# One decoder layer on one core: in the first segment, keys and values transposed by TensorE, and 1/rms applied as results leave PSUM

## The chip, the cores and the metric

The kernel runs on one core of one Trainium2 chip. Five engines of the core have a queue each and work it off in order: TensorE (PE in the profile, with its weight loads as PEld), VectorE (DVE), ScalarE (ACT), GpSimd (POOL) and SyncE (SP), which here only issues DMAs. Matmul results land in PSUM, everything else lives in SBUF. The metric is the device time of one launch in microseconds.

## The reference

One layer, 2048 tokens, width 1024. The input is normalised, projected once, split into two groups of heads that each run a chunked recurrence, gated, and projected back:

```python
h = rms_norm(x, attn_norm)                      # x * rsqrt(mean(x*x) + EPS) * gain
proj = h @ w_in                                 # 1024 -> 8216 columns
(mq, mk, mv, mo, mz, mi, mf, gqkv, gz, gb, ga) = split(proj)
h_m = mlstm_chunkwise(q_m, k_m, v_m, i_pre, f_pre)          # 4 heads, q/k 128, v 256
y_m = rms(h_m) * sigmoid(mo) * silu(mz)
qkv = silu(causal_depthwise_conv(gqkv, g_conv))             # 8 heads of 128, conv of 4 taps
q_g, k_g, v_g = l2_norm(gq), l2_norm(gk), gv
o_g = gated_delta_chunkwise(q_g, k_g, v_g, log_alpha, beta) # triangular solve per chunk, state 128x128
y_g = rms(o_g) * silu(gz)
x = x + concat(y_m, y_g) @ w_out
out = rms_norm(x, final_norm)
```

What matters here: every projection of the normalised input is the projection of (x times gain) multiplied by one number per token, 1/rms. It can be multiplied into the input before, or into the result after. And the gated-delta heads need keys and values both with the channel on the partitions (as the projection and the convolution give them) and with the token on the partitions (for the state update), so they are transposed.

## The kernel before

The tokens go in four **segments** of 512, each of four chunks of 128. A segment is eight **windows**, written out in `ORDER`: P0, M0, P1, M1, P2, M2, P3, M3. A P window projects queries, keys, values and gate of a pair of gated-delta heads (`g_proj`), an M window those of one mLSTM head (`m_proj`). The generator `window` takes the steps of these projections as a filler and puts between them, at given fractions of the window, the steps of other streams: `prep` of pair n (the chunk matrices and a 32-step forward substitution) in window M n; `level` (building the 128x128 inverse), the first part of `chain` (the recurrence over the chunks) of pair n and `m_chunks` of head n in window P n+1; the rest of `chain` in window M n+1. PE runs in exactly the order in which the program is written. On DVE, ACT, POOL and SP a scheduler sets the order, from priorities and a simulated timeline of its own.

Every product of a projection is three passes (`hi*hi + hi*lo + lo*hi` of fp32 split in two). `proj_fm` (L337) makes 128 columns of a weight with the channel on the partitions, one PSUM tile of 128x512 from three buffers of `psj`; `proj_tm` (L365) makes 256 columns with the token on the partitions, four tiles of 128x256. In the first segment the weights come raw from HBM and are split on the way: a cast on ACT (L175) and a subtraction on POOL (L177), and both halves are written back to HBM, from where the other segments load them.

Also in the first segment alone, `raw[0]` is true: `hh` and `hl` hold x times gain without 1/rms. The result is therefore multiplied while it stands in PSUM, and read out after that: in `proj_fm` by DVE with `rbc0` (L348, 1/rms broadcast along the partitions), in `tm_done` by ACT with the column `rs0` (L361). Then the consumer reads PSUM: `keep_v` copies the mLSTM values to `mv` on ACT (L508) and DVE makes the low half `vlo` (L511); `conv_silu` copies to `xin` on ACT (L662), makes the first tap on ACT from PSUM (L664) and the other three on DVE (L666); `mq` and `mk` are copied on ACT (L498, L499); `mo` goes through tanh on ACT (L515).

The tables `VT` and `KTR` say for each segment (first, middle ones, last) and pair who transposes: 1 means DVE, in 16 blocks of four 32x32 transposes each for a head (`to_tokens`, L484), directly behind `conv_silu`, for the values (`gv`) and the keys (`ktok`); 0 means PE, four or two 128x128 transposes at a time into PSUM tiles of the pool `psc` (5 buffers), for the keys in `g_prep` (`ktp`, L736, read by ACT for the squares and a copy, L739 and L741) and for the values in `g_chain` (`vp`, L919, read by ACT, L921). Both go through `by_dve`. In the first segment pair 0 has 0 in both tables, pairs 1 to 3 have 1.

Names that come later: `dmz`, `zp`, `fp`, `zq`, `E` belong to `level`; `SS` is the state of the recurrence, `sp`, `vq`, `su`, `op` are its matmuls; `pts` and `kws` are split operands of `m_chunks`, `CN` and `nd` its state and output; `kl` are low halves for `prep`.

Of the kernel before, what the change touches and what calls it, by code (L numbers as in the profile page):

```python
# [10 lines left out]
F32 = mybir.dt.float32  # L11
# [40 lines left out]
VT = ((0, 1, 1, 1), (1, 1, 1, 1), (1, 0, 0, 0))  # L52
KTR = ((0, 1, 1, 1), (1, 1, 1, 1), (0, 1, 0, 0))
# [12 lines left out]
def hybrid_layer(  # L66
# [160 lines left out]
    rs0 = cst.tile([P, NCH], F32, name="rs0")  # L227
    rbc0 = cst.tile([P, T], F32, name="rbc0")
# [109 lines left out]
    def proj_fm(w, c0, nm, done):  # L338
# [3 lines left out]
        for k in range(KT):  # L342
# [3 lines left out]
            if k == KT - 1:  # L346
                if raw[0]:
                    nc.vector.tensor_tensor(ps, ps, rbc0, op=ALU.mult)  # L348
                done(ps)
# [9 lines left out]
    def tm_done(ps, t, done):  # L359
        if raw[0]:  # L360
            nc.scalar.activation(ps, ps, AF.Copy, scale=rs0[:, t:t + 1])  # L361
        done(ps, t)

    def proj_tm(w, nm, done):

        n = w[0][0].shape[-1]
        for t in range(NCH):
            ps = psj.tile([P, T], F32, tag="pj", name=f"pt_{nm}_{t}")[:, 0:n]
            for k in range(KT):
                tm_step(ps, w, t, k)  # L370
# [117 lines left out]
    def m_proj(seg, n, r):  # L488
# [9 lines left out]
                           lambda ps: nc.scalar.activation(qT, ps, AF.Copy, scale=DK ** -0.5))  # L498
        yield from proj_fm(w, P, f"mk{s_}", lambda ps: nc.scalar.copy(kT, ps))  # L499
# [6 lines left out]

        def keep_v(ps, t):
            nc.scalar.copy(vt[:, t, 0:256], ps)  # L508
            if fast:
                with tc.high_priority(VPR):  # L510
                    nc.vector.tensor_tensor(vlo[:, t, :], ps, vt[:, t, 0:256].bitcast(F32),  # L511
                                            op=ALU.subtract)
        yield from proj_tm(w, f"mv{s_}", keep_v)
        w = next_w()
        yield from proj_tm(w, f"mo{s_}", lambda ps, t: nc.scalar.activation(  # L515
            G[:, t, :], ps, AF.Tanh, scale=0.5))
# [133 lines left out]
    def g_proj_qkv(seg, pr, r):  # L650
        s_ = f"{seg}_{pr}"
        for part, tag in ((1, "gk"), (0, "gq"), (2, "gv")):
            w = next_w()
            for j in range(2):
# [715 lines left out]
```

## Time and profile before

| what | value |
|---|---|
| time, median of 3 runs | 2358.06 us (2354.9 to 2360.65) |
| profiled execution, its own time | 2354.22 us |
| span of its trace | 2352.2 us |
| PE busy | 2225.8 us (95%), 14750 matmuls |
| DVE busy | 1925.3 us (82%) |
| ACT busy | 876.1 us (37%) |
| POOL busy | 714.5 us (30%) |

The page's slices of the span read: PE 8 and 9 tenths from the start on and 9 everywhere behind the first quarter; DVE between 7 and 9; the granted clock 9 tenths in the first slices. The first segment ends at 534.5 us, where the projection `pt_gz` of the second one starts. Its windows begin at 7.5 (P0), 67.2 (M0), 134.4 (P1), 206.3 (M1), 265.9 (P2), 335.7 (M2), 395.6 (P3) and 465.5 us (M3); those of the second segment at 534.5, 603.0, 662.2, 724.1, 779.3, 836.5, 891.2 and 948.3 us. A view by stretches over these bounds gives one line for a window, with the busy time of each engine and the granted clock as a share of full speed.

### The profile page before, as it was taken

The numbers are of one execution on the slowest core, as the hardware profiler recorded it, in microseconds if no ns is written. First come the engines' busy times: TensorE is split into PE (matmuls) and PEld (weight loads), VectorE is DVE, ScalarE is ACT, GpSimd is POOL, SyncE is SP. The second block draws the span as 40 slices with busy tenths as digits, with TensorE's granted clock in tenths as the row PEclk, the third lists the DMA queues.
The fourth block names the chain that finished last, engine by engine and source line by source line (L and its number), as shares of the span: only waits on it lengthen the run. The fifth ranks groups of instructions, "written<-read, shape, count | busy, mean of one in ns | idle before, by whom it ended". The sixth has DMA issues, their size and how long they took to land.

```text
span 2352.2 us, 41574 instructions
## 1 busy us (share of the span) xinstructions
PE 2225.8 (95%) x14750; PEld 1970.7 (84%) x14750; DVE 1925.3 (82%) x5359; ACT 876.1 (37%) x2351; POOL 714.5 (30%) x820
## 2 busy tenths in 40 slices
PE   8889899889899999998999999999999999999998
PEld 7778788788789898887898989888988997777777
DVE  7989898996988888879888888788766837988784
ACT  5535454544333434343333343443334234111111
POOL 4435353451302121413020214130212114444433
PEclk9889999999999999999999999999999999999999
DMA  7766657574445554645454556454546455222221
GB/s 254 249 204 233 233 188 245 184 267 156 163 155 182 171 194 168 223 155 174 155 182 158 191 176 232 146 182 157 183 169 205 166 194 159 73 99 90 99 81 63
DMA packets 183320, 409.18 MB, mean 174 GB/s; under 512 B 51736, under 2 KB 84632, under 8 KB 183112
## 3 DMA queue, kind: packets, MB, share of 16 engines
q1 hardware_dynamic: 182392, 405.74, 50.9%
q8 instruction: 116, 1.90, 0.3%
q14 instruction: 92, 0.75, 0.1%
q10 hardware_dynamic: 720, 0.79, 0.1%
HBM read 309.68 MB, written 96.90 MB: 173 GB/s over the span
## 4 chain that ended last, share of the span: by engine, by line
PE 45%; DVE 37%; DMA 6%; issue 5%; ACT 3%; POOL 3%; SPq 0%; POOLq 0%; ACTq 0%; DVEq 0%
DVE ytt L1185 6%; DVE ktok L484 3%; DVE tb L816 3%; DVE xb L820 3%; DVE gv L484 2%; DVE kw L484 2%; PE pt_mz L355 2%; PE pt_mz L356 2%; PE pt_mz L357 2%; PE pt_mo L355 2%; PE pt_mo L356 2%; PE pt_mo L357 2%; PE pt_gz L356 2%; PE pt_gz L355 2%; PE pt_gz L357 2%
## 5 line engine op out<-in xcount | busy, mean ns | idle before, releaser
L1185 DVE STREAM_TRANSPOSE ytt<-yl 32x256 f32<-32x256 f32 x448 | 195.1, 436 | 42.0 <-POOL ylo L1153 35.9
L816 DVE TENSOR_TENSOR tb<-xb,lbt 128x248 f32<-128x248 f32 (+30 forms) x496 | 181.2, 365 | 20.5 <-DMA lbt<-l_d 7.7
L820 DVE TENSOR_TENSOR xb<-xb,tb 128x248 f32<-128x248 f32 (+30 forms) x496 | 172.0, 347 | 12.7
L983 POOL TENSOR_TENSOR gms<-gms,nhalf 128x2 f32<-128x2 f32 x64 | 46.8, 730 | 421.9 <-DVE gms L981 421.5
L355 PE MATMUL pt_mv<-whi_M,hh 128*128 128x256 f32 x512 | 149.3, 292 | 12.4 <-DVE vlo L511 8.3
L355 PE MATMUL pt_gz<-whi_P,hh 128*128 128x256 f32 (+1 forms) x512 | 153.8, 300 | 2.8 <-ACT whi_P L175 1.7
L355 PE MATMUL pt_mz<-whi_M,hh 128*128 128x256 f32 x512 | 150.1, 293 | 5.6 <-DVE tz L522 4.8
L355 PE MATMUL pt_mo<-whi_M,hh 128*128 128x256 f32 x512 | 149.4, 292 | 4.3 <-DVE vlo L511 4.3
L357 PE MATMUL pt_gz<-whi_P,hl 128*128 128x256 f32 (+1 forms) x512 | 148.3, 290 | 1.5 <-DVE mr L630 1.5
L356 PE MATMUL pt_gz<-wlo_P,hh 128*128 128x256 f32 (+1 forms) x512 | 148.4, 290 | 1.4 <-DVE wlo_P L177 1.4
L356 PE MATMUL pt_mv<-wlo_M,hh 128*128 128x256 f32 x512 | 145.9, 285 | 0.0
L357 PE MATMUL pt_mv<-whi_M,hl 128*128 128x256 f32 x512 | 145.8, 285 | 0.0
L357 PE MATMUL pt_mz<-whi_M,hl 128*128 128x256 f32 x512 | 145.8, 285 | 0.0
L356 PE MATMUL pt_mz<-wlo_M,hh 128*128 128x256 f32 x512 | 145.8, 285 | 0.0
L357 PE MATMUL pt_mo<-whi_M,hl 128*128 128x256 f32 x512 | 144.7, 283 | 0.0
L356 PE MATMUL pt_mo<-wlo_M,hh 128*128 128x256 f32 x512 | 144.6, 282 | 0.0
L1233 ACT ACTIVATE jkf<-xr 128x512 f32<-128x512 f32 (+1 forms) x33 | 20.5, 620 | 278.5 <-DVE xr L1231 144.9
L484 DVE STREAM_TRANSPOSE ktok<-gk 32x128 f32<-32x128 f32 x384 | 116.1, 302 | 5.4
L484 DVE STREAM_TRANSPOSE gv<-xingv 32x128 f32<-32x128 f32 x384 | 116.0, 302 | 5.4
L1226 PE MATMUL po<-woh,ylo 128*128 128x512 f32 (+1 forms) x297 | 115.1, 388 | 0.6 <-POOL ylo L1153 0.6
L1224 PE MATMUL po<-woh,yh 128*128 128x512 f32 (+1 forms) x297 | 114.5, 386 | 0.9 <-ACT yh L1152 0.9
L1225 PE MATMUL po<-wol,yh 128*128 128x512 f32 (+1 forms) x297 | 114.7, 386 | 0.2 <-POOL wol L1032 0.2
(403 smaller groups left out, 7535.9 us busy)
## 6 DMA issues: line engine op xcount, KB each, us to landing
whi_M<-wdM SPq DMA_DIRECT2D x96, 512.0 KB, 3.9
wlo_M<-wdM SPq DMA_DIRECT2D x96, 512.0 KB, 5.3
whi_P<-wdP SPq DMA_DIRECT2D x90, 512.0 KB, 3.8
wlo_P<-wdP SPq DMA_DIRECT2D x90, 512.0 KB, 5.0
wraw_M<-in_wg_dram SPq DMA_DIRECT2D x32, 512.0 KB, 6.8
wdM<-whi_M SPq DMA_DIRECT2D x32, 512.0 KB, 3.0
wdM<-wlo_M SPq DMA_DIRECT2D x32, 512.0 KB, 5.7
wraw_P<-in_wg_dram SPq DMA_DIRECT2D x30, 512.0 KB, 6.0
```

The costliest lines, as they stand in the source:

```text
L355: nc.tensor.matmul(ps, lhsT=hh[k][:, ts], rhs=hi, start=(k == 0), stop=False)
L356: nc.tensor.matmul(ps, lhsT=hh[k][:, ts], rhs=lo, start=False, stop=False)
L357: nc.tensor.matmul(ps, lhsT=hl[k][:, ts], rhs=hi, start=False, stop=(k == KT - 1))
L484: nc.vector.transpose(dst[32 * a:32 * a + 32, :, 32 * b:32 * b + 32], s4[32 * b:32 * b + 32, :, a, :])
L816: nc.vector.tensor_tensor(tb[:, :, 0:n], xb[:, :, i:i + 1].broadcast_to([P, 8, n]), lbt[:, i:i + 1, i + 1:32].broadcast_to([P, 8, n]), op= ...
L820: nc.vector.tensor_tensor(xs, xs, tb[:, :, 0:n], op=ALU.subtract)
L983: nc.gpsimd.tensor_tensor(ms, ms, nhalf[:, 0:2], op=ALU.pow)
L1185: nc.vector.transpose(ytt[32 * b:32 * b + 32, :, 32 * a:32 * a + 32], y3[32 * a:32 * a + 32, :, 32 * b:32 * b + 32])
L1224: nc.tensor.matmul(ps, lhsT=yh, rhs=woh, start=(k == 0), stop=False)
L1225: nc.tensor.matmul(ps, lhsT=yh, rhs=wol, start=False, stop=False)
L1226: nc.tensor.matmul(ps, lhsT=ylo, rhs=woh, start=False, stop=(k == 15))
L1233: nc.scalar.activation(jk[:, 0:n], xr[:, cs], AF.Square, accum_out=ssf[:, i:i + 1])
```

## The change

In the first segment all pairs now have 0 in both tables, so keys and values of pairs 1 to 3 are transposed by PE too. And 1/rms is no longer multiplied in PSUM: the instruction that takes the result out of PSUM applies it. `fm_out` does so on DVE for `mq`, `mk` and `xin`; `keep_v` and the tanh of `mo` take the column as ACT's scale, and `vlo` takes it as DVE's scalar. The first tap of the convolution then reads `xin` and not PSUM. `gz` and `mz` keep the multiplication in PSUM. A new column `rs0h` holds half of `rs0`.

```diff
-VT = ((0, 1, 1, 1), (1, 1, 1, 1), (1, 0, 0, 0))
-KTR = ((0, 1, 1, 1), (1, 1, 1, 1), (0, 1, 0, 0))
+VT = ((0, 0, 0, 0), (1, 1, 1, 1), (1, 0, 0, 0))
+KTR = ((0, 0, 0, 0), (1, 1, 1, 1), (0, 1, 0, 0))
...
+        nc.vector.tensor_scalar_mul(rs0h, rs0, 0.5)
...
             if k == KT - 1:
-                if raw[0]:
-                    nc.vector.tensor_tensor(ps, ps, rbc0, op=ALU.mult)
                 done(ps)
...
+    def fm_out(dst, ps, scale=None):
+        if not raw[0]:
+            if scale is None:
+                nc.scalar.copy(dst, ps)
+            else:
+                nc.scalar.activation(dst, ps, AF.Copy, scale=scale)
+        elif scale is None:
+            nc.vector.tensor_tensor(dst, ps, rbc0, op=ALU.mult)
+        else:
+            nc.vector.scalar_tensor_tensor(dst, ps, scale, rbc0, op0=ALU.mult, op1=ALU.mult)
...
-    def tm_done(ps, t, done):
-        if raw[0]:
+    def tm_done(ps, t, done, scaled=True):
+        if raw[0] and scaled:
             nc.scalar.activation(ps, ps, AF.Copy, scale=rs0[:, t:t + 1])
         done(ps, t)
...
         def keep_v(ps, t):
-            nc.scalar.copy(vt[:, t, 0:256], ps)
+            if raw[0]:
+                nc.scalar.activation(vt[:, t, 0:256], ps, AF.Copy, scale=rs0[:, t:t + 1])
+            else:
+                nc.scalar.copy(vt[:, t, 0:256], ps)
...
+                        nc.vector.scalar_tensor_tensor(
+                            vlo[:, t, :], ps, rs0[:, t:t + 1], v_, op0=ALU.mult, op1=ALU.subtract)
...
-            G[:, t, :], ps, AF.Tanh, scale=0.5))
+            G[:, t, :], ps, AF.Tanh, scale=rs0h[:, t:t + 1] if raw[0] else 0.5), False)
...
-                    nc.scalar.copy(xi[:, 3:T + 3], ps)
+                    fm_out(xi[:, 3:T + 3], ps)
...
-                    nc.scalar.activation(d, ps, AF.Copy, scale=conv_c[:, fi, 3:4])
+                    nc.scalar.activation(d, xi[:, 3:T + 3] if raw[0] else ps, AF.Copy,
+                                         scale=conv_c[:, fi, 3:4])
```

Lines of the changed kernel are some 20 higher in the orders below (L484 is the block transpose of before; L666 has become L687, L890 L911, L971 L992, L736 L757).

Order on DVE in window P2, from the second key projection to the transpose `dmz` that PE waits for; `kws` belongs to `m_chunks`. Before:

```order
L348 TENSOR_TENSOR pf_gk_2_1_3036<-pf_gk_2_1_3036,rbc_174 128x512
L577 SCALAR_TENSOR_TENSOR kws_1_nm<-kw_1_3144,ws_748,kws_1_pt 128x128
L484 STREAM_TRANSPOSE ktok_2_0_3018<-gk_2_0_2981 32x4x32 x2
...
L484 STREAM_TRANSPOSE ktok_2_0_3018<-gk_2_0_2981 32x4x32 x8
L666 SCALAR_TENSOR_TENSOR gk_2_1_3035<-xingk_2_1_3087,conv_c,gk_2_1_3035 128x512
L890 STREAM_TRANSPOSE dmz<-E_241 32x8x32
```

The same place in the changed kernel:

```order
L367 TENSOR_TENSOR xingk_2_1_2984<-pf_gk_2_1_2934,rbc_175 128x512
L597 SCALAR_TENSOR_TENSOR kws_1_nm<-kw_1_3024,ws_745,kws_1_pt 128x128 x4
L687 SCALAR_TENSOR_TENSOR gk_2_1_2933<-xingk_2_1_2984,conv_c,gk_2_1_2933 128x512 x3
L911 STREAM_TRANSPOSE dmz<-E_242 32x8x32
```

The sixteen block transposes ahead of `dmz` are gone, and two more taps of the convolution stand ahead of it.

Order on DVE at the end of window P2, from the second value projection to the state update `SS` that PE waits for. Before:

```order
L348 TENSOR_TENSOR pf_gv_2_1_3431<-pf_gv_2_1_3431,rbc_174 128x512
L630 TENSOR_SCALAR mr_1_2_3459<-mr_1_2_3459 128x1
L484 STREAM_TRANSPOSE gv_2_0_3339<-xingv_2_0_3404 32x4x32 x6
L617 SCALAR_TENSOR_TENSOR CN_247<-CN_247,dec_754,up_1_3_3535 128x258
...
L770 TENSOR_TENSOR kl_2_1_pt<-gk_2_1_3035,kh_2_1_3812 128x2x128
L770 TENSOR_TENSOR kl_2_1_nm<-gk_2_1_3035,kh_2_1_3812 128x2x128
L484 STREAM_TRANSPOSE gv_2_0_3339<-xingv_2_0_3404 32x4x32 x4
L770 TENSOR_TENSOR kl_2_0_3805<-gk_2_0_2981,kh_2_0_3804 128x2x128 x2
L971 COPY SS_252<-su_1_0_3591 128x128
```

The same place in the changed kernel:

```order
L367 TENSOR_TENSOR xingv_2_1_3364<-pf_gv_2_1_3295,rbc_175 128x512
L637 SCALAR_TENSOR_TENSOR CN_248<-CN_248,dec_751,up_1_3_3385 128x258
L791 TENSOR_TENSOR kl_2_1_pt<-gk_2_1_2933,kh_2_1_3677 128x2x128
L791 TENSOR_TENSOR kl_2_1_nm<-gk_2_1_2933,kh_2_1_3677 128x2x128
L791 TENSOR_TENSOR kl_2_0_3670<-gk_2_0_2897,kh_2_0_3669 128x2x128 x2
L992 COPY SS_253<-su_1_0_3441 128x128
```

Again sixteen block transposes (six, six and four) have left the stretch.

Order on PE at the start of window M2, behind the recurrence's `vq`. Before, `pf_mq` follows at once; in the changed kernel:

```order
L970 MATMUL vq_1_1_3594<-R_1_1_3510,E_242 128x128 x2
L940 MATMUL vp_1_2_3600<-ident,gv_1_0_1763 128x128
L940 MATMUL vp_1_2_3600<-ident,gv_1_1_1840 128x128
L757 MATMUL ktp_2_0_3626<-ident,gk_2_0_2897 128x128 x4
L345 MATMUL pf_mq_2_3587<-hh,whi_M_2_0_0_3409 128x512
```

Two value transposes and four key transposes have come in. In all PE has 48 more: six groups of four (`ktp`) and twelve of two (`vp`); apart from them its order is as it was. DVE has 192 block transposes fewer, and `rs0h` more.

## Rows read from the trace of the kernel before

**Rows 1.** By stretches, first segment: P1, M1, P2, P3, M3 (columns in line one)
```profile
core 0: us, PE busy (x) PEld busy (x) DVE busy (x) ACT busy (x) POOL busy (x), PEclk, DMA share, GB/s
134.40:206.30 71.90, 62.03 (x398) 53.20 (x398) 62.31 (x157) 33.91 (x81) 27.86 (x33) 0.90 0.55 184
206.30:265.90 59.60, 55.77 (x422) 52.84 (x421) 55.46 (x158) 29.23 (x86) 27.71 (x16) 1.00 0.72 244
265.90:335.70 69.80, 61.17 (x396) 51.90 (x395) 61.29 (x152) 35.44 (x89) 30.73 (x33) 0.90 0.57 198
...
395.60:465.50 69.90, 60.12 (x395) 51.42 (x394) 61.30 (x150) 34.70 (x86) 30.79 (x33) 0.93 0.56 195
465.50:534.50 69.00, 60.97 (x428) 57.47 (x427) 66.55 (x163) 33.20 (x92) 38.20 (x28) 0.93 0.71 247
```

**Rows 2.** By stretches, second segment: P1, M1, P2, M3
```profile
662.20:724.10 61.90, 60.09 (x407) 51.80 (x407) 52.72 (x152) 27.71 (x74) 10.16 (x23) 0.94 0.42 147
724.10:779.30 55.20, 54.57 (x417) 52.25 (x417) 44.27 (x156) 14.40 (x49) 9.28 (x10) 1.00 0.57 196
779.30:836.50 57.20, 56.81 (x406) 49.19 (x406) 51.39 (x148) 26.55 (x68) 10.18 (x23) 1.00 0.47 157
...
948.30:1011.10 62.80, 58.72 (x428) 55.42 (x427) 52.98 (x143) 21.15 (x62) 25.15 (x23) 0.97 0.67 222
```

**Rows 3.** PE's waits, 134.4 to 534.5 us: total us, times, longest us
```profile
PE sp L940 <- DVE SS L971: 9.7, 3, 3.8
PE fp L884 <- ACT dmz L879: 7.6, 2, 4.2
PE zq L895 <- DVE dmz L890: 5.5, 3, 3.4
PE zp L875 <- DVE dmz L869: 4.0, 2, 2.6
PE sp L940 <- DVE SS L973: 3.8, 1, 3.8
PE pt_mv L355 <- DVE vlo L511: 3.8, 2, 2.0
```

**Rows 4.** PE's waits, 662.2 to 1011.1 us, same windows of the second segment
```profile
PE vq L949 <- DVE R L943: 3.8, 3, 2.4
PE zq L895 <- DVE dmz L890: 2.6, 3, 1.8
PE sp L940 <- DVE SS L973: 1.0, 2, 0.6
```

**Rows 5.** DVE by line, 134.4 to 534.5 us: busy us, mean ns | idle before
```profile
L484 DVE STREAM_TRANSPOSE ktok<-gk 32x128 f32<-32x128 f32 x96 | 29.0, 302 | 1.3
L484 DVE STREAM_TRANSPOSE gv<-xingv 32x128 f32<-32x128 f32 x96 | 29.0, 302 | 1.2
...
L553 DVE TENSOR_TENSOR pts<-ptt,pts 128x512 fp32r<-128x512 f32 x3 | 7.3, 2437 | 0.6 <-ACT pts L552 0.5
```

**Rows 6.** DVE by line, second segment's window P2
```profile
L553 DVE TENSOR_TENSOR pts<-ptt,pts 128x512 fp32r<-128x512 f32 x1 | 0.7, 693 | 0.0
```

**Rows 7.** DVE in order of time, end of P2: start us, us
```profile
326.14 1.26 DVE L484 STREAM_TRANSPOSE gv<-xingv 32x128 f32<-32x128 f32 x4
...
328.11 0.48 DVE L971 COPY SS<-su 128x128 f32<-128x128 f32 x2
```

**Rows 8.** PE in order of time, window M0 (pair 0's keys)
```profile
73.84 0.60 PE L736 MATMUL ktp<-ident,gk 128*128 128x128 f32 x4
74.20 0.48 PE L343 MATMUL pf_mq<-hh,whi_M 128*128 128x512 f32 x1
```

**Rows 9.** PE, one line: ns min/median/max, first and last start us
```profile
L919 PE MATMUL vp<-ident,gv x8: 271/272/273, 178.0 to 231.8; 128*128 128x128 f32 x8
```

**Rows 10.** ACT by line, 0 to 534.5 us
```profile
L361 ACT ACTIVATE pt_mo<-pt_mo,rs 128x256 f32<-128x256 f32 x16 | 7.2, 447 | 18.6 <-PE pt_mo L357 15.7 <-DVE xb L820 2.9
...
L662 ACT COPY xingq<-pf_gq 128x512 f32<-128x512 f32 x8 | 4.7, 587 | 14.7 <-DVE pf_gq L348 14.7
```

More of the change, by code (lines that the diff above doesn't have):

```diff
@@ L227, in hybrid_layer @@
     rs0 = cst.tile([P, NCH], F32, name="rs0")
+    rs0h = cst.tile([P, NCH], F32, name="rs0h")
     rbc0 = cst.tile([P, T], F32, name="rbc0")
@@ L357, in tm_step, with proj_tm @@
         nc.tensor.matmul(ps, lhsT=hl[k][:, ts], rhs=hi, start=False, stop=(k == KT - 1))
-    def tm_done(ps, t, done):
-        if raw[0]:
+    def fm_out(dst, ps, scale=None):
[10 more added lines that the diff above has]
+        if raw[0] and scaled:
             nc.scalar.activation(ps, ps, AF.Copy, scale=rs0[:, t:t + 1])
         done(ps, t)
-    def proj_tm(w, nm, done):
+    def proj_tm(w, nm, done, scaled=True):
         n = w[0][0].shape[-1]
@@ L371, in proj_tm @@
                 if k == KT - 1:
-                    tm_done(ps, t, done)
+                    tm_done(ps, t, done, scaled)
                 yield 0.33
@@ L497, in m_proj @@
         yield from proj_fm(w, 0, f"mq{s_}",
-                           lambda ps: nc.scalar.activation(qT, ps, AF.Copy, scale=DK ** -0.5))
-        yield from proj_fm(w, P, f"mk{s_}", lambda ps: nc.scalar.copy(kT, ps))
+                           lambda ps: fm_out(qT, ps, DK ** -0.5))
+        yield from proj_fm(w, P, f"mk{s_}", lambda ps: fm_out(kT, ps))
         w = next_w()
@@ L507, in keep_v @@
         def keep_v(ps, t):
-            nc.scalar.copy(vt[:, t, 0:256], ps)
+            if raw[0]:
+                nc.scalar.activation(vt[:, t, 0:256], ps, AF.Copy, scale=rs0[:, t:t + 1])
+            else:
+                nc.scalar.copy(vt[:, t, 0:256], ps)
             if fast:
+                v_ = vt[:, t, 0:256].bitcast(F32)
                 with tc.high_priority(VPR):
-                    nc.vector.tensor_tensor(vlo[:, t, :], ps, vt[:, t, 0:256].bitcast(F32),
-                                            op=ALU.subtract)
-        yield from proj_tm(w, f"mv{s_}", keep_v)
+                    if raw[0]:
+                        nc.vector.scalar_tensor_tensor(
+                            vlo[:, t, :], ps, rs0[:, t:t + 1], v_, op0=ALU.mult, op1=ALU.subtract)
+                    else:
+                        nc.vector.tensor_tensor(vlo[:, t, :], ps, v_, op=ALU.subtract)
+        yield from proj_tm(w, f"mv{s_}", keep_v, False)
         w = next_w()
         yield from proj_tm(w, f"mo{s_}", lambda ps, t: nc.scalar.activation(
-            G[:, t, :], ps, AF.Tanh, scale=0.5))
+            G[:, t, :], ps, AF.Tanh, scale=rs0h[:, t:t + 1] if raw[0] else 0.5), False)
         w = next_w()
```

## The prediction

> **What bounds the kernel now.** I read the stretches first. PE is the engine that the time follows: it is busy for 95% of the span, and in the second segment a window lasts little longer than PE's work in it, 57.2 us for 56.81 in P2 at a granted clock of 1.00 [rows 2]. In the first segment this isn't so. P2 takes 69.8 us with 61.17 busy, at 0.90 of full speed, and PE's work is itself longer for the lower clock; DVE is busy for 61.29, where it has 51.39 in the second segment's P2 [rows 1, 2]. The six windows from P1 to M3 last 400.1 us (134.4 to 534.5), and the same six of the second segment 348.9 (662.2 to 1011.1). That gap of 51.2 us is the most that relief of the first segment can be after, since the two do the same products.
>
> Next I read what PE waits for there. Six kinds make 34.4 us: 9.7 + 7.6 + 5.5 + 4.0 + 3.8 + 3.8, all but one directly on DVE, and that one (`fp`) on an ACT copy of something that DVE transposed [rows 3]. In the same windows of the second segment three kinds make 7.4 [rows 4]. So DVE's lateness at the points where PE needs a result is the cost, and not its busy share as such.
>
> The third reading is what DVE does there. The block transposes of keys and values are 192 instructions, 29.0 + 29.0 us [rows 5]. They stand in front of the awaited results: at the end of P2 they run until 327.4, `SS` starts at 328.11 behind two low halves, and PE, which waits for it, starts at 328.45 [rows 7], one of the three waits of up to 3.8 [rows 3]. DVE is also slowed by POOL: the 128x512 operation with two inputs in SBUF (L553) takes 2437 ns against 693 in the second segment [rows 5, 6], where POOL has 10 us of work in that window rather than 31 [rows 1, 2]. The transposes have 302 ns whoever runs beside them.
>
> **The change part by part.** *Transposes off DVE.* It loses 58.0 us, 19.3 for each of three pairs. P1 and M1 together are 62.31 + 55.46 = 117.8 of DVE work in 131.5 us; without it 98.5, close to the 97.0 in 117.1 of the second segment's P1 and M1 [rows 1, 2]. What counts are the waits. Before `dmz` of `level` in a P window sixteen key blocks leave (16 x 0.302 = 4.8 us), before `SS` sixteen value blocks, more than the longest wait in each place (4.2, 3.4, 3.8). Kind by kind [rows 3]: `SS` L971 all 9.7; `fp` 6 of 7.6; `zq` 5 of 5.5; `zp` nothing of 4.0, since both waits end at 151 and 154 us, ahead of the first block transpose; `SS` L973 in M3 2 of 3.8, since other DVE work is late there too; `vlo` 3 of 3.8 (with the ACT pass below). Together 25.7 us.
>
> *The clock.* A window's length times the missing share of the clock gives what PE's slower running costs: P1 71.9 x 0.10 = 7.2, P2 7.0, P3 4.9, M3 4.8, together 23.9 [rows 1]; in the second segment P1 3.7 and M3 1.9, together 5.6, and P2 nothing [rows 2]. The windows below full speed are those where PE waits; M1, with few waits, has 1.00. If the first segment comes to the second's state, 23.9 - 5.6 = 18.3 us come back; I take 18. This overlaps the waits little, since PE idles in a wait whatever its clock.
>
> *Transposes on PE.* 48 come in: six groups of four and twelve of two. Four of pair 0 hold PE from 73.84 to 74.20, 0.09 us each, and its next matmul starts without idle time [rows 8]. Forty-eight make 4.3; another 0.09 for each of 18 groups for the change of operands, an estimate, 1.6. The cost is 5.9 us, wholly on the path. The value groups stand before `sp` in the recurrence, and pair 0's ran so without a lengthened duration, 271 to 273 ns for all eight [rows 9]. The results need a reader out of PSUM, and it is ACT, which has 34 us of work in a 72-us window [rows 1]: six copies of `ktp` more, at 0.6 each 3.6 us. The values were read by an ACT copy before too, only out of SBUF.
>
> A page of the Trainium skill speaks against this part: "TensorE: Matmul & The Clock Gate", Part 4, says that a transpose doesn't count as busy PE for the clock. Here M1 holds two of the value groups (starts 208 and 231.8 us) and its granted clock is 1.00 [rows 1, 9], so the trace doesn't bear it out for short groups among projections. What it would give is a rival below.
>
> *1/rms on the way out.* DVE's multiplications stay as many, with SBUF as the output in place of PSUM. ACT loses 32 scalings at 447 ns and 32 copies at 587, 14.3 + 18.8 = 33.1 us [rows 10]. It is not the engine waited for, so nearly all of this lies beside other work; what is worth something is one ACT step less between a product and the release of its buffer. For `mv` the step of 0.447 stood before `vlo`, for which PE waited twice (counted above). For the projections with three buffers of `psj` none of the six kinds stands in the list [rows 3], so the earlier release is worth nothing. Against it, the first tap now follows the write of `xin`, where it followed the multiplication in PSUM before: the same place in the chain. For the write into SBUF no row of before stands; bounds are -2 us (POOL's work delays it, as it does L553) and +4 (all of ACT's steps that remain in waits of level and `vlo`). I take +1, nearer to nothing, since ACT has slack of half a window.
>
> *Holds.* The block transposes were the DVE work that POOL doesn't slow. POOL is busy for 27.86 of 71.9 us in P1, 39% [rows 1], so of 19.3 us per pair some 7.5 lay beside it, 22 in all, and two-input work now takes that place: DVE gets back less than 58 us. "GPSIMD Engine Reference", section 1 (Specifications), of the Trainium skill states the same of such DVE instructions, and names the interface to SBUF that the two engines share; the 2437 against 693 ns agree [rows 5, 6]. Only what reaches PE is a loss. Bounds are 0 (DVE has 33 us of slack per pair) and 22; I take 2.5, near to nothing, since the `dmz` and `SS` steps are small ones with one input and merely queue behind a held one (some 1.7 us longer, half of them in a place where PE waits, three pairs).
>
> *Other queues.* POOL and SP issue what they issued, and apart from order within a window nothing moves past a DMA. With PE faster the weights of the first segment are wanted sooner; the windows M1 and M2, 59.6 us at 1.00, show that POOL and DMA (share 0.72) can supply a window at that pace [rows 1].
>
> Sum: 25.7 + 18 + 1 - 5.9 - 2.5 = 36.3. The profiled execution took 2354.22, so 2317.9; the median of the runs is 3.8 above it, so the forecast for a median is 2358.06 - 36.3 = 2321.8, as a round number **2321 us**. A second way agrees: the gap between the segments, 51.2, less 5.9 for the transposes, is 45.3, if nothing else kept the first segment slower. POOL's weight subtraction, raw loads and holds do keep it slower, so that is the upper end and not the middle.
>
> **The rivals.** *Part of the relief is taken back (B).* PE runs in program order, and when it no longer waits for `SS` it gets to the next dependency of the same chain sooner: `R`, `kl`, `CN`. The second segment, with less held DVE work, still has 7.4 us of waits with `R` first among them [rows 4]. If half of the 25.7 us turns into such waits and half of the 18 of clock stays lost with them, 12.9 + 9 + 1 - 5.9 - 2.5 = 14.5 us are left: 2344. For it speaks L553's price; against it that DVE's load falls to the second segment's. Its reach is a gain of 10 to 26.
>
> *Transposes starve the clock (the page's rule).* If a window that holds them isn't granted full speed, P windows keep their 0.90 (18 us not gained) and M1 and M2 go from 1.00 to 0.90 (59.6 x 0.10 = 6.0 each, 12 in all): 36.3 - 30 = 6, so 2352. Against it stands M1's 1.00 with two groups in it.
>
> *Nothing moves (C).* The waits go, and PE then stands at weights from POOL or at `zp`-like waits with the same total; 5 us or less, 2358. It wants all of 25.7 + 18 eaten; unlikely with DVE 19 us lighter for each pair.
>
> *Slower (D).* PE is in order, and the 18 groups now wait in its queue for the data (`gv` and `gk` out of the convolution and a silu) and for one of five `psc` buffers, which `prep`, `level` and the chain use too. If each of the twelve value groups waited as long as the longest wait of now, 3.8 us [rows 3], that would be 45.6 us against a gain of 36: some 9 slower, 2367. It decides from about 3.0 us per group on (36.3 / 12). Against it: none of the six kinds is a wait of pair 0's `vp` or `ktp` in this same segment, and the values are ready a window before.
>
> **How the numbers follow.** The forecast (a gain of 26 to 50, 2308 to 2332) has 0.66: its main terms are waits whose cause is seen ahead of them. B has 0.18, the clock rule 0.03, nothing 0.06, slower 0.07. The clock rule's 6 us of gain count as faster by a hair. For 8 in 10 the range takes in the forecast and B but for its far end: 2306 to 2346. That holds the bounds of the 1/rms term, and of the holds nearly all (22 would leave a gain of 17). A measurement can tell 0.2%, 4.7 us, from no change. Faster 0.66 + 0.18 + 0.03 = 0.87, within 0.06, slower 0.07.
>
> **What the changed profile would show.** Right: P2 at 58 to 60 us and a clock of 0.98 or more, P3 alike; DVE busy for 98 to 106 us in P1 and M1 together; `SS` L971's and `zq`'s successors gone from PE's waits or under 1 us a piece; P1's `zp` waits of 4 us still there; M1 and M2 at some 57 to 60. For B: P2 at 63 or more, and new waits for `R`, `kl` or `CN`, with two-input DVE rows of over 1.5 us. For the clock rule: M1 below 0.95 with no wait to explain it. For D: waits before `vp` or `ktp`. If the M windows get longer by over 3 us each, the PE term was too small. The forecast fails as a whole if DVE's rows for xin (128x512, now into SBUF) are much longer than the multiplication in PSUM was.

## The result, and the profile after

The changed kernel takes 2328.36 us, median of 4 runs (2327.45 to 2330.98), where the kernel before took 2356.48 beside it: 0.9881 of the time, 95% interval 0.9863 to 0.9899, 28.1 us faster. The forecast was 37 us, to 2321. The profiled execution took 2328.85 us, its span 2327.1.

The stretches of the changed kernel are read first, P0 to M3 of the first segment, the columns as in [rows 1].

```profile
7.49:71.00 63.51, 53.49 (x261) 44.14 (x261) 56.35 (x100) 32.81 (x59) 25.19 (x22) 0.92 0.81 280
71.00:135.81 64.81, 55.45 (x377) 52.27 (x376) 59.55 (x137) 27.61 (x71) 28.86 (x20) 0.90 0.65 230
135.81:200.17 64.36, 58.87 (x399) 50.20 (x397) 52.01 (x98) 30.07 (x72) 28.39 (x32) 0.95 0.59 207
200.17:261.82 61.65, 57.82 (x429) 55.27 (x429) 52.35 (x146) 26.60 (x76) 29.57 (x17) 0.97 0.73 241
261.82:320.06 58.24, 56.70 (x400) 48.51 (x398) 52.20 (x100) 32.85 (x80) 29.02 (x33) 1.00 0.66 230
320.06:381.25 61.19, 58.08 (x428) 55.33 (x429) 51.72 (x147) 26.37 (x76) 29.44 (x17) 0.97 0.72 243
381.25:439.19 57.94, 56.45 (x400) 48.45 (x398) 51.90 (x100) 32.79 (x79) 29.52 (x32) 1.00 0.67 230
439.19:511.81 72.62, 61.79 (x439) 58.19 (x440) 60.86 (x150) 30.90 (x84) 39.15 (x28) 0.95 0.70 235
```

Against [rows 1], P1, P2 and P3 are shorter by 7.5, 11.6 and 12.0 us, 31.1 together, and P2 and P3 run at full clock. M1 and M3 are longer by 2.1 and 3.6 (M2, 59.98 before, by 1.2). P0 and M0, 59.7 and 67.2 before, together grew by 1.4. From P1 to M3 the kernel takes 376.0 us where it took 400.2, a gain of 24.2; the second segment begins 22.7 us earlier, and a few us more appear in it. Of the 24.2 us, 18.1 are time in which PE does nothing (44.4 before, 26.3 now), and 6.1 are a shorter busy time (355.8 to 349.7), although 40 of the 48 transposes that came to PE lie in these windows.

What PE waits for from P1 to M3, in the columns of [rows 3]:

```profile
PE vq L970 <- DVE R L964: 12.9, 4, 5.0
PE fp L905 <- ACT dmz L900: 4.8, 1, 4.8
PE sp L961 <- DVE SS L994: 2.6, 1, 2.6
...
PE zq L916 <- DVE dmz L911: 0.8, 2, 0.5
```

Of [rows 3] the waits for `SS` L971 and `zp` are gone from the list, and `zq` is down to 0.8. New is 12.9 us for `R`, the step behind `sp` in the same recurrence. In the kernel before this kind had 2.5 us in the same windows.

What stands ahead of `R` in M3, where PE waits longest: DVE in order of time (start us, us, instruction, and in brackets the idle time before it).

```profile
461.58 0.68 DVE L367 TENSOR_TENSOR mk<-pf_mk,rbc 128x512 f32<-128x512 f32 x1
462.18 2.74 DVE L557 SCALAR_TENSOR_TENSOR ptt<-nm,ccol,negmask 128x128 f32<-128x128 f32 x2
464.85 5.04 DVE L496 STREAM_TRANSPOSE kw<-mk 32x128 f32<-32x128 f32 x16
469.92 0.61 DVE L964 SCALAR_TENSOR_TENSOR R<-sp,neg,vr 128x128 f32<-128x128 f32 x2
```

GpSimd in the same stretch:

```profile
462.29 2.48 POOL L177 TENSOR_TENSOR wlo_M<-wraw_M,whi_M 128x1024 fp32r<-128x1024 f32 x1 [1.04 <-ACT whi_M L175]
```

Two suspects stand there together: block transposes again (those of the mLSTM keys, which the change left on DVE), and `ptt`, whose pair of instructions takes 2.74 us beside GpSimd's weight subtraction, where the pair before it takes 0.91. In M1 and M2 a substitution step of 2.4 us stands 2 to 3 us ahead of `R`, beside a GpSimd subtraction as well, and no transpose.

### The profile page after: what moved, and what is told of

Read it like the earlier page. It is cut to its first block, busy times and chain, and to the rows that moved or that the text cites. A ratio compares the mean times of both kernels' runs of the same rounds, so it can differ in the third digit from the quotient of the medians.

```text
span 2327.1 us, 41431 instructions
## 1 busy us (share of the span) xinstructions
PE 2219.4 (95%) x14798; PEld 1967.5 (85%) x14798; DVE 1886.3 (81%) x5168; ACT 855.0 (37%) x2293; POOL 716.7 (31%) x820
## 4 chain that ended last, share of the span: by engine, by line
PE 50%; DVE 32%; DMA 6%; issue 5%; POOL 3%; ACT 3%; SPq 1%; POOLq 0%; ACTq 0%; DVEq 0%
DVE ytt L1206 7%; DVE tb L837 3%; DVE xb L841 3%; DVE ktok L496 2%; PE pt_mz L355 2%; PE pt_mz L356 2%; PE pt_mz L357 2%; PE pf_gv L345 2%; PE pf_gv L346 2%; PE pf_gv L347 2%; PE pt_mo L355 2%; PE pt_mo L357 2%; PE pt_mo L356 2%; PE pt_gz L356 2%; PE pt_gz L357 2%
## 5 line engine op out<-in xcount | busy, mean ns | idle before, releaser
L841 DVE TENSOR_TENSOR xb<-xb,tb 128x248 f32<-128x248 f32 (+30 forms) x496 | 171.6, 346 | 12.9
L345 PE MATMUL pf_gq<-hh,whi_P 128*128 128x512 f32 x256 | 107.5, 420 | 0.0
L355 PEld LDWEIGHTS pt_mv<-whi_M,hh 128*128 128x128 f32 x512 | 98.3, 192 | 10.4 <-DVE vlo L529 4.7
```

Of the source, the lines that this page charges most:

```text
L345: nc.tensor.matmul(ps, lhsT=hi[k // HK][:, k % HK, c0:c0 + P], rhs=hh[k], start=(k == 0), stop=False)
L355: nc.tensor.matmul(ps, lhsT=hh[k][:, ts], rhs=hi, start=(k == 0), stop=False)
L841: nc.vector.tensor_tensor(xs, xs, tb[:, :, 0:n], op=ALU.subtract)
```

## The experiments

The two halves were first run alone, then the two suspects. Each edit is one to the kernel that is named in its expectation; the kernel before ran beside every group, with medians from 2355.73 to 2357.19.

**The tables alone.** The edit:

```
-VT = ((0, 1, 1, 1), ...     +VT = ((0, 0, 0, 0), ...
-KTR = ((0, 1, 1, 1), ...    +KTR = ((0, 0, 0, 0), ...
```

> The kernel before with only the two tables changed in the first segment: keys and values of pairs 1 to 3 transposed by TensorE, 1/rms still multiplied in PSUM. The whole change gained 28.1 us (2356.48 to 2328.36). Theory T (the block transposes in front of awaited results were the cost, as the sum had it): 24 to 30 us faster than before, P2 and P3 at 58 to 60 us. Rival S (much of the gain is that ACT and PSUM are relieved by 1/rms on the way out): 8 to 16 us faster, P2 at 63 or more.

2335.9 us beside 2356.15: 20.3 faster, ratio 0.9917 (0.9902 to 0.9932). Less than theory T had, more than its rival. P1, P2 and P3 take 63.0, 64.5 and 62.6 us, not 58 to 60. PE's waits from P1 to M3:

```profile
PE fp L884 <- ACT dmz L879: 8.8, 2, 4.4
PE sp L940 <- DVE SS L973: 5.2, 1, 5.2
PE pt_mv L355 <- DVE vlo L511: 4.8, 2, 2.4
PE vq L949 <- DVE R L943: 4.7, 4, 2.0
```

`SS` L971 is gone and `zq` is down to 0.6, as the sum had it. `zp` still has 3.8. But `fp`, of whose 7.6 us it gave 6 to the transposes, has 8.8 without them, and `SS` L973, `vlo` and `R` have grown.

**1/rms alone.** The changed kernel with the two tables of the kernel before:

```
-VT = ((0, 0, 0, 0), ...     +VT = ((0, 1, 1, 1), ...
-KTR = ((0, 0, 0, 0), ...    +KTR = ((0, 1, 1, 1), ...
```

> The kernel before with only 1/rms applied on the way out of PSUM; the block transposes stay on VectorE. Theory T: worth about 1 us, the time between 3 us faster and 4 us slower than before, P2 still near 70 us. Rival S: 8 us faster or more. If the stretch P0 and M0, 1.4 us longer in the changed kernel, belongs to this half, it shows here too: P0 at 63 us for 59.7 before.

2348.53 beside 2356.15: 7.6 faster, ratio 0.9974 (0.9965 to 0.9983). This falls between the two expectations and far outside the +1 of the sum. The two halves make 20.3 + 7.6 = 27.9, the whole 28.1: the times add up. The waits don't: from P1 to M3 this run has 2.1 us for `SS` L971 (9.7 before, none in the list with the tables alone), so either half by itself takes most of that wait away; `zp` and the wait of `pt_mv` for `vlo` are in the list with the tables alone (3.8 and 4.8) and not in this one; `zq` stays at 6.3 and needs the tables; `fp` has 9.3, and `R` 6.3 for 2.5. The longer P0 is of this half (64.4 us).

**GpSimd's subtraction in pieces.** The weights of the first segment are split by a subtraction of 128x1024 on GpSimd; here it is four of 128x256. The same loop also cuts eight subtractions of the first weights, which DVE makes in P0. PE's order is the same, DVE's differs in some 150 rows of over 10,000 in the two lists together.

```
-            eng.tensor_tensor(lo[:, ks, :], raw_[:, ks, :], hi[:, ks, :]..., op=ALU.subtract)
+            for q in range(k0, k0 + step):
+                eng.tensor_tensor(lo[:, q:q+1, :], raw_[:, q:q+1, :], hi[:, q:q+1, :]..., op=ALU.subtract)
```

> The changed kernel, with GpSimd's subtraction for the low half of a raw weight made in four pieces of 128x256 in place of one of 128x1024 (2.4 us). In the changed kernel TensorE waits 12.9 us for R in four waits, 6.6 for a cq copy, and VectorE's substitution steps, the copy of 128x32 and others take up to 2.4 us beside such a subtraction. Theory H (holds by GpSimd decide these waits): a held instruction is held for 0.6 us or so, the waits for R fall to 6 us or less and that for cq below 5; 5 to 12 us faster than the changed kernel. Rival O (VectorE's order decides: R stands behind other work): waits as they are, time within 3 us of the changed kernel, or slower by what twelve more GpSimd instructions for each weight cost.

2306.24 us, ratio 0.9793 (0.9778 to 0.9808) to the kernel before: 22.1 us faster than the changed kernel, almost twice the upper end of what theory H gave. Cutting the subtractions is worth that much, and more than was expected. It isn't that the weights come sooner: from P0 to M3 PE waits 3.4 us for them in the changed kernel and 3.3 here. But the waits for `R` did not fall (12.2 us), so that part of theory H failed with this run; the gain came elsewhere. P0 and M0 have 115.7 us together for 128.3, P1 60.5 for 64.4, M1 58.6 for 61.65; P1 to M3 make 10.4 us of it, and P0 and M0 12.6, where the forecast did not look.

P0 shows how. In the changed kernel PE waits 6.6 us there for `cq`, and three instructions on DVE's way to it are each lengthened by some 2.2 us:

```profile
51.40 3.52 DVE L421 TENSOR_TENSOR_SCAN rt<-ones,u 12x128 f32<-12x128 f32 x4
...
60.03 2.86 DVE L693 SCALAR_TENSOR_TENSOR gq<-xingq,gq 128x512 f32<-128x512 f32 x1
...
65.44 2.35 DVE L447 COPY cq<-gt 128x32 f32<-128x32 f32 x1
```

In the kernel before the same three take 1.35, 0.69 and 0.17 us. The first is no new loss: there the scan behind it (`ew`, 4x512) is lengthened in its place, 3.43 us for 1.25 here. The other two make 4.4 us, and the wait for `cq` grew from 2.1 to 6.6. GpSimd ran a subtraction beside each of them (beside the first from 51.48 us); those beside the last two:

```profile
59.98 2.37 POOL L177 TENSOR_TENSOR wlo_M<-wraw_M,whi_M 128x1024 fp32r<-128x1024 f32 x1 [0.60 <-ACT whi_M L175]
...
65.41 2.34 POOL L177 TENSOR_TENSOR wlo_M<-wraw_M,whi_M 128x1024 fp32r<-128x1024 f32 x1
```

The copy starts 0.03 us behind a subtraction and ends 0.04 us behind its end. With four pieces it takes 0.46 us, and the wait for it is 1.8.

```profile
62.20 0.46 DVE L449 COPY cq<-gt 128x32 f32<-128x32 f32 x1
```

**The mLSTM keys transposed by TensorE too.** ScalarE and VectorE read the keys out of PSUM:

```
-MT = ((1, 1, 1, 1), ...     +MT = ((0, 0, 0, 0), ...
-        if fast or by_dve(MT, seg, h):
+        if by_dve(MT, seg, h):
...
+            if fast:
+                kw = ktp.rearrange("p (c j) -> p c j", c=NCH)
```

> The changed kernel, with the mLSTM keys of the first segment too transposed by TensorE (four 128x128 into one PSUM tile for each of four heads) and their consumers reading PSUM. VectorE loses 64 block transposes, 19 us; TensorE gets 16, about 2 us. In the changed kernel sixteen of them (5.04 us) stand right in front of R in M3, where TensorE waits 4.98 us, and fourteen in M0 in front of vlo (wait of 4.54). Theory T2 (what is left of the loss is again block transposes): 5 to 10 us faster than the changed kernel, M3 at 68 us or less. Rival H (the waits for R come from holds by GpSimd): M1 and M2 keep their waits of 2.5 and 3.1, and the whole is 0 to 4 us faster or up to 2 slower.

2327.96 us, ratio 0.9882 (0.9865 to 0.99): no difference to the changed kernel. M3 is 4.0 us shorter (68.6, where theory T2 had 68 or less), yet P1 is 3.0 longer, the second segment's P0 3.9 longer (69.0 for 65.1, at a clock of 0.95 for 1.00), and the waits for `R` are still 8.9. Taking another 64 block transposes, 19 us, off DVE bought nothing in all, where the first 192 bought 20: they do stand in the way of `R` in M3, but what is won there is lost elsewhere, for a cause that is open. The second suspect is left.

**Pieces in the kernel before.** The same edit as above, on the kernel before.

> The kernel before (transposes on VectorE, 1/rms in PSUM) with only GpSimd's weight subtractions in four pieces. In the changed kernel this edit gained 22 us (2328.4 to 2306.2). Theory A (the holds and the block transposes are separate costs, added up): before gains about as much, 18 to 24 us, and the block transposes still cost some 28 us on top. Theory B (the block transposes sheltered VectorE from the holds: in the changed kernel 82 us of its work from P1 to M3 was lengthened against 71 in the one before): before gains less, 10 to 16 us. Theory C (the waits of before that the sum laid to the block transposes were holds as well): before gains more than the changed kernel did, 26 us or more, and the change would then be worth less than 24 us with pieces.

2333.01 beside 2355.73: 22.7 faster, ratio 0.99 (0.9885 to 0.9915). By the total this is theory A: pieces are worth as much with the block transposes on DVE as without them, and with pieces the change is worth 2333.01 - 2306.24 = 26.8 us, for 28.1 without. By windows it is not. Here P1 to M3 are 17.6 us shorter (382.6 for 400.2) and P0 and M0 3.5; in the changed kernel it was 10.4 and 12.6. In P1 to M3, the windows that the sum is about, the change is thus worth 17.0 us with pieces (382.6 to 365.6) and 24.2 without: there the two costs overlap, the way theory C has it, and the equal totals are a coincidence of two different places. `SS` L971 has 7.4 us of waits for 9.7, `zq` 3.3 for 5.5 and `fp` 4.6 for 7.6 in [rows 3], with all transposes still on DVE, and `R` has 6.3. For `fp` the trace of the kernel before shows that it is not a matter of the transposes. ScalarE there, in P2, up to the `dmz` that `fp` needs:

```profile
279.97 0.63 ACT L670 ACTIVATE xingk<-gk 128x512 f32<-128x512 f32 x1
282.65 1.28 ACT L576 ACTIVATE kws_pt<-kw,ws 128x128 fp32r<-128x128 f32 x4 [2.05 <-DVE pts L553]
283.85 1.12 ACT L175 CAST whi_P<-wraw_P 128x512 fp32r<-128x512 f32 x2
284.88 0.57 ACT L662 COPY xingk<-pf_gk 128x512 f32<-128x512 f32 x1
285.35 0.68 ACT L664 ACTIVATE gk<-pf_gk,conv_c 128x512 f32<-128x512 f32 x1
286.06 0.76 ACT L879 COPY dmz<-zp 32x256 f32<-32x256 f32 x2
```

`zp` was ready at 281.6, and its copy stands in ScalarE's queue behind `kws_pt`. That one waited 2.05 us for `pts` on DVE, and `pts` was held by GpSimd:

```profile
280.10 2.52 DVE L553 TENSOR_TENSOR pts<-ptt,pts 128x512 fp32r<-128x512 f32 x1 [0.53 <-ACT pts L552]
```

```profile
279.68 2.39 POOL L177 TENSOR_TENSOR wlo_P<-wraw_P,whi_P 128x1024 fp32r<-128x1024 f32 x1 [3.29 <-ACT whi_P L175]
```

This is the L553 of [rows 5], which the prediction had read as a price of holds and not connected to `fp`. In the changed kernel `fp` waits in P1 instead, for a `dmz` that stands behind a cast which waited 2.67 us for its weight's DMA:

```profile
152.72 0.62 ACT L175 CAST whi_P<-wraw_P 128x512 fp32r<-128x512 f32 x1 [2.67 <-DMA wraw_P<-in_wg_dram]
```

**TensorE's transposes issued twice.** A loop around the 48 that the change brought, for `vp` and `ktp` alike:

```
+                    for _ in range(2 if seg == 0 and pr else 1):
-                    nc.tensor.transpose(vp[:, j * P:(j + 1) * P], ...
+                        nc.tensor.transpose(vp[:, j * P:(j + 1) * P], ...
```

> The changed kernel with each of the 48 transposes that came to TensorE issued twice, into the same place. The sum had 5.9 us for 48 (0.09 each and as much again for each group). If that is right, 4 to 7 us slower than the changed kernel. If a transpose costs more than its pitch (a group delays the chain, or starves the clock), 10 us or more. If the groups lie in gaps anyway, under 3 us.

2329.96 us, ratio 0.9886 (0.9872 to 0.9901): 1.6 us above the changed kernel, within what either varies. By the two intervals the difference can lie some 5 us to either side of that, so 10 us or more is ruled out, and 5.9 isn't told from nothing. The trace has the work: from P1 to M3, where 40 of them lie, PE is busy for 353.1 us and not 349.7, and idle for 23.1 and not 26.3, in a stretch of 376.2 for 376.0. They have 272 ns each, beside other matmuls:

```profile
L758 PE MATMUL ktp<-ident,gk 128*128 128x128 f32 x56 | 7.4, 272 | 0.0
L942 PE MATMUL vp<-ident,gv 128*128 128x128 f32 x40 | 6.4, 273 | 0.0
```

**The half of 1/rms for `mv` and `mo`.** On the kernel before, ScalarE's scaling in PSUM falls away for these two alone:

```
-            nc.scalar.copy(vt[:, t, 0:256], ps)
+            nc.scalar.activation(vt[:, t, 0:256], ps, AF.Copy, scale=rs0[:, t:t + 1])
...
-            G[:, t, :], ps, AF.Tanh, scale=0.5))
+            G[:, t, :], ps, AF.Tanh, scale=rs0h[:, t:t + 1] if raw[0] else 0.5), False)
```

> The kernel before with only the values' and the output gate's part of the 1/rms edit: ScalarE's scaling pass in PSUM falls away for mv and mo (32 passes of 447 ns), the rest still multiplied in PSUM. The whole 1/rms edit alone gained 7.6 us (2356.15 to 2348.53), where the sum had 1. If the gain is the shorter step ahead of vlo and the freed PSUM tiles of mv and mo, this half has most of it: 5 to 8 us faster. If it lies with the convolution's inputs and with mq and mk, this half is worth 0 to 3 us.

2355.38 beside 2355.73, ratio 0.9998 (0.9988 to 1.0009): nothing. It is not the step of 447 ns ahead of `vlo`: the wait of `pt_mv` for it falls from 3.8 to 0.2, that of `pt_mo` rises from 1.6 to 3.0, and the time stays.

**Pieces and keys together.** The edits of both runs above, on the changed kernel.

> The changed kernel with both: weight subtractions in four pieces, and the mLSTM keys of the first segment transposed by TensorE. The second alone gained nothing (2327.96 for 2328.36). If that was because holds set the time of the awaited steps, the keys now bring something: 3 to 8 us faster than pieces alone (2306.2), with M3 at 67 us or less. If VectorE's lateness in M windows is only the order of its queue, nothing: within 2 us of 2306.

2305.99 us, ratio 0.9786 (0.977 to 0.9801), 0.25 from pieces alone. In the total the block transposes that are left don't matter even with shorter holds. In the trace the first segment ends 6.9 us earlier than with pieces alone (482.4 for 489.3; M3 has 69.1), but the second segment's P0 takes 3.5 us more (68.1 for 64.6, at 0.95 for 1.00), as in the run with the keys alone; why is open.

**Two and eight pieces.** With two:

```
+            for q in range(k0, k0 + step, 2):
+                eng.tensor_tensor(lo[:, q:q+2, :], raw_[:, q:q+2, :], hi[:, q:q+2, :]..., op=ALU.subtract)
```

With eight, each of the four is cut at `ncol // 2` again.

> The changed kernel with GpSimd's weight subtractions in two pieces of 128x512 (some 1.2 us each) in place of one of 2.4. Four pieces gained 22.1 us (2328.4 to 2306.2). Theory H (the length of a hold sets the price): between, 10 to 18 us faster than the changed kernel. If what counted in four pieces was something else (weights ready earlier, a luckier order), no ladder: near 0 or near the whole 22.

> The same in eight pieces of 128x128. With four pieces GpSimd's busy time for these subtractions rose from 140 to 188 us, since a quarter took 802 to 894 ns and not 600. Theory H with that overhead: holds get shorter still, but there are more of them and GpSimd is busy longer; near the four pieces, 16 to 24 us faster than the changed kernel. If VectorE lost in proportion to GpSimd's busy time, it would be worse than four pieces by 5 us or more.

2319.94 us (ratio 0.9846, 0.9828 to 0.9864) and 2313.18 (0.9811, 0.9793 to 0.9829). From one piece to eight the times are 2328.4, 2319.9, 2306.2 and 2313.2 us. Two gained 8.4, a little under the 10 expected; eight gained 15.2, under four. GpSimd's rows, from P1 to M3, with one, two, four and eight pieces:

```profile
L177 POOL TENSOR_TENSOR wlo_M<-wraw_M,whi_M 128x1024 fp32r<-128x1024 f32 x24 | 57.8, 2417 | 37.1 <-ACT whi_M L175 35.5 <-PE pt_mv L357 1.1
...
L179 POOL TENSOR_TENSOR wlo_M<-wraw_M,whi_M 128x512 fp32r<-128x512 f32 x48 | 63.8, 1353 | 31.5 <-ACT whi_M L175 31.4
...
L179 POOL TENSOR_TENSOR wlo_M<-wraw_M,whi_M 128x256 fp32r<-128x256 f32 x96 | 72.9, 793 | 38.8 <-ACT whi_M L175 32.9 <-PE pt_mo L359 6.0
...
L179 POOL TENSOR_TENSOR wlo_M<-wraw_M,whi_M 128x128 fp32r<-128x128 f32 x192 | 91.5, 516 | 31.5 <-ACT whi_M L175 31.5
```

The busy time rises from 57.8 to 91.5 us while the single piece gets shorter, from 2.4 to 0.5. The lowest of these four times lies between the two. Two pieces are clear of one and of four. Eight are 6.9 us above four, the number that went with a loss in proportion to GpSimd's busy time, but the two ran beside different runs of the kernel before, and by their ratios to the kernel before it is 4.2 us with intervals that overlap: whether eight are worse than four is not settled. And a pair of substitution steps costs DVE less there than with four pieces (403 + 401 = 804 ns for 834, mean of the rows read as below), which speaks against that reading. P0, P1 and M1 are the windows that are longer than with four (63.2 for 57.4, 63.9 for 60.5, 61.5 for 58.6), and DVE's order differs too; if there is a loss, its cause stays open.

**No subtraction on GpSimd.** ScalarE writes the low half:

```
+            if eng is nc.gpsimd:
+                for q in range(k0, k0 + step, 2):
+                    nc.scalar.copy(lo[:, q:q + 2, :], raw_[:, q:q + 2, :])
```

> The changed kernel with GpSimd's weight subtraction left out: ScalarE writes the low half as a second copy of the raw weight, so the products are not the reference's. It takes 58 pieces of 2.4 us off GpSimd and puts 116 casts of some 0.57 us on ScalarE. Theory H (what is left in the first segment's M windows, the waits for R of 12 us among them, are substitution steps held by GpSimd): 28 to 40 us faster than the changed kernel, waits for R under 5 us. If the remaining waits are the order of VectorE's queue: no better than four pieces, 18 to 24 us, waits for R near 12.

2285.29 us, ratio 0.9696 (0.9678 to 0.9714): 43.1 us faster than the changed kernel, above the range expected. Not all of it need be holds: GpSimd has 140 us less to do, and the low halves come from another engine. From P1 to P3 all five windows take 56.0 to 56.9 us, those with TensorE's transposes in them too. M1 and P2:

```profile
175.38:231.83 56.45, 56.01 (x431) 53.65 (x430) 41.65 (x144) 34.85 (x92) 8.23 (x7) 1.00 0.76 260
231.83:287.87 56.04, 56.04 (x399) 48.38 (x398) 40.21 (x101) 40.79 (x96) 12.04 (x26) 1.00 0.68 242
```

PE is busy in all of P2, at full clock, and one kind of wait is left from P1 to M3:

```profile
PE vq L974 <- DVE R L968: 5.6, 4, 2.4
```

The substitution steps show what DVE got back. `tb` in the kernel before (first), after (second) and without the subtraction (third), P1 to M3, busy us and mean ns:

```profile
L816 DVE TENSOR_TENSOR tb<-xb,lbt 128x64 f32<-128x64 f32 (+30 forms) x101 | 53.6, 531 | 2.7
...
L837 DVE TENSOR_TENSOR tb<-xb,lbt 128x32 f32<-128x32 f32 (+30 forms) x97 | 46.6, 481 | 2.6
...
L841 DVE TENSOR_TENSOR tb<-xb,lbt 128x16 f32<-128x16 f32 (+30 forms) x95 | 32.1, 338 | 2.5
```

The mean mixes shapes, but it is the same mix within a few instructions. The other half of a step, `xb`, went from 391 ns before to 451 after and 346 without the subtraction: taken together a pair costs 922, 932 and 684 ns. With four pieces it is 409 + 425 = 834. So four pieces leave 150 of the 248 ns by which a pair is longer than without the subtraction. That fits the waits for `R`, which stayed at 12 us with four pieces and fell to 5.6 (under 5 was expected) without the subtraction.

**The convolution's half of 1/rms.** On the kernel before:

```
+                    if raw[0]:
+                        nc.vector.tensor_tensor(xi[:, 3:T + 3], ps, rbc0, op=ALU.mult)
+                    else:
                     nc.scalar.copy(xi[:, 3:T + 3], ps)
...
-                    nc.scalar.activation(d, ps, AF.Copy, scale=conv_c[:, fi, 3:4])
+                    nc.scalar.activation(d, xi[:, 3:T + 3] if raw[0] else ps, AF.Copy, scale=conv_c[:, fi, 3:4])
```

> The kernel before with only the convolution's inputs (xin) multiplied on the way out of PSUM by VectorE and the first tap read from xin; mq, mk, mv and mo as before. The whole 1/rms edit gained 7.6 us, the part of mv and mo 0.4. If the convolution (24 of ScalarE's 32 copies, and the earlier release of psj) carries it: 5 to 8 us faster than before. If mq and mk carry it: 0 to 3 us.

2347.9 beside 2357.19: 9.3 faster, ratio 0.9965 (0.9948 to 0.9982). The convolution carries the whole of it, as far as the intervals tell. ScalarE's step between product and first tap is gone (`xin`, 587 ns), and the buffer of `psj` is free after DVE's instruction, not after ScalarE's tap. PE's waits from P1 to M3 in this kernel:

```profile
PE fp L888 <- ACT dmz L883: 8.5, 3, 4.2
PE zq L899 <- DVE dmz L894: 6.6, 3, 3.3
...
PE pt_gz L355 <- DVE xingv L663: 3.6, 2, 2.2
PE sp L944 <- DVE SS L977: 3.4, 1, 3.4
PE vq L953 <- DVE R L947: 2.4, 1, 2.4
PE sp L944 <- DVE SS L975: 2.0, 3, 1.6
```

`SS` L975, the L971 of [rows 3], has 2.0 us where it had 9.7, with all the block transposes still on DVE; `zp` is not in the list; `fp` and `zq` stand there undiminished; 3.6 us of a new wait, for `xingv`, has come. Which of the shorter chain and the earlier release brings the gain was not tried apart, and stays open.

## Why the prediction was nearly right, point by point

**The sign, the place and P2 and P3** were right: 58.24 and 57.94 us for 58 to 60 forecast, at a clock of 1.00; DVE's 52.01 + 52.35 = 104.4 us in P1 and M1 lies in 98 to 106; `SS` L971 left PE's waits and `zq` nearly. The time is inside the range, 9 us short of the forecast gain. Two signs failed: M1 and M2, given 57 to 60 us, took 61.65 and 61.19, and P1's waits for `zp`, which should have stayed, are gone.

**The waits that go** were sized well as a sum and wrongly by kind. The six kinds of [rows 3] fell from 34.4 to 8.2 us (4.8 + 2.6 + 0.8), 26.2 for the 25.7 forecast. That the sums agree is luck. Only `zq` went as reasoned, with the transposes and only with them. `SS` L971 went with them too, but 1/rms alone takes 7.6 of its 9.7, and pieces alone 2.3. `fp` fell with neither half alone, since its ScalarE copy stands behind `pts`, which GpSimd holds, or behind a weight's cast. And `zp`, given nothing, went with the convolution's part of 1/rms, which had no such term.

**The step that failed** is the one that took no new wait into the forecast. Waits for `R` rose from 2.5 to 12.9 us, 10.4 taken back, at the very place that rival B named, `R` first. Its price was set at 14.5 us left of the gain; the truth lies between B and the forecast, in the M windows: M1 and M2, which the forecast held at 57 to 60 us, and M3, for which it named no length and which took 72.62 us for 69.0 before.

**The holds** had 2.5 us in the sum, within bounds of 0 to 22, because the awaited `dmz` and `SS` steps have one input and merely queue behind a held one. Of these two rows it is true: in the first segment of either kernel `dmz` takes 432 to 438 ns and the `SS` copy 273 to 285. But the queueing isn't cheap (`fp`, `R`), and in P0, outside the frame, an awaited copy with one input was itself held, `cq`, 2.35 us for 0.17. Their whole price in the changed kernel is at most 43 us (no subtraction on GpSimd), and pieces of a quarter won 22. What the change itself added to them no run shows by itself: pieces are worth 22.7 us before it and 22.1 behind it, but 17.6 and 10.4 from P1 to M3, and 3.5 and 12.6 in P0 and M0. The forecast's frame, in which DVE is late because of the transposes, left the holds out of the wait for `fp`, out of the waits for `SS` and `zq`, which pieces alone lower by 2.3 and 2.2, and out of P0 and M0.

The Trainium skill, "GPSIMD Engine Reference", section 1 (Specifications), names two-input DVE instructions and those in a 2-port mode; the rows agree for the former (L553, L557), and the one-input copy of 128x32 that took 2.35 us would be of the latter kind, which no run here shows apart.

**The clock.** The lost share by window is P1 64.4 x 0.05 = 3.2, M1 and M2 61.65 x 0.03 and 61.19 x 0.03, 1.8 each, M3 72.6 x 0.05 = 3.6: 10.5 us from P1 to M3, for 23.9 before. So 13.4 came back and not 18; M1 and M2 went from 1.00 to 0.97. The forecast's reckoning also multiplies whole windows, waits included, so that waits and clock are in part counted twice. Over PE's busy time alone (62.03 x 0.10 and so on) the loss is 20.8 before and 9.5 after, 11.3 back, and the forecast's 18.3 would have been 15.4.

**TensorE's transposes** had 5.9 us, wholly on the path. As work this is about right: PE's busy time times the granted clock, summed over P1 to M3, is 335.0 us before, 340.2 in the changed kernel and 346.4 with the transposes doubled (estimates, from rounded clocks), 5 to 6 us for the 40 that lie there, where the sum's prices give 4.9. On the path it was less in the one trace of the doubled kernel, in which PE's idle time fell by 3.2 us as its busy time rose by 3.4; the medians, 1.6 us apart, settle neither.

**The rule on the clock** (a rival with 0.03) is not borne out: P2 and P3 went from 0.90 and 0.93 to 1.00 with transposes in them, and with the transposes doubled M1 and P2 are granted 1.00 each. The groups fill only some 1 to 2 us of a window, so this says nothing of longer runs of transposes.

```profile
197.15:258.14 60.99, 57.26 (x437) 54.70 (x437) 51.62 (x144) 26.72 (x76) 29.80 (x17) 1.00 0.72 242
258.14:317.43 59.29, 57.21 (x403) 48.98 (x401) 51.91 (x99) 32.69 (x80) 29.11 (x33) 1.00 0.65 227
```

**1/rms** had +1 with bounds of -2 to 4 and measured 7.6: its upper bound was too low. The sentence that failed is that the first tap stands "the same place in the chain" and that an earlier release of `psj` is worth nothing as long as no wait of the list names it. The part that was priced, the 447 ns ahead of `vlo`, is worth nothing. By halves the forecast was 35 and 1 (32 and 4 with `vlo` counted here) and the chip gave 20.3 and 7.6. So the tables gave some 12 to 15 us less than forecast and 1/rms 4 to 7 more; that the total came within 9 us owes something to the one making up for part of the other.

**Slower (D)** did not come: no wait of `vp` or `ktp` is in PE's list.

## What to carry to other kernels

When work is taken off a late engine, the waits that it caused go, but the engine that waited comes to the next dependency of the same chain sooner; look what stands ahead of that one in the queue, and take part of the gain off. Before a wait is laid to the work in front of the awaited step, ask of each row there whether it is of its usual length, and follow the queue of the engine in between: `fp` waited for ScalarE, ScalarE for VectorE, and VectorE for GpSimd. A long GpSimd instruction beside a busy VectorE is worth cutting before anything is moved: four pieces gave 22 us in either kernel, though in different windows, and with the change 2306.2 us, 50 below the kernel before.

## What the runs showed of the hardware

A VectorE copy of 128x32 with one input in SBUF, 0.17 us by itself, took 2.35 us when it started beside a GpSimd subtraction of 2.34, and a scan over 12 partitions was lengthened likewise (one of four took 2.55, and the four 3.52 for 1.35). In none of the traces was one of VectorE's 128x512 multiplications that read PSUM longer than 0.70 us, or one of the transposes of four 32x32 blocks longer than 0.31, whatever GpSimd did. GpSimd's subtraction of 128x1024 takes 2.4 us, a quarter of it 0.79 and an eighth 0.52: cut into eight, the busy time is 1.6 times as long (91.5 for 57.8 us). A 128x128 transpose on TensorE takes 272 ns; windows that hold them were granted 1.00 (P2 and P3, and M1 and P2 with twice as many), and where less was granted (M1 and M2, 0.97) PE also waited for `R`.
